# The branch products of a hybrid trunk layer in bursts of half-size products

## The chip, the core and the metric

The kernel runs on one core of a Trainium2 chip. The metric is the device time in microseconds of one execution. The core has TensorE (PE) for matmuls, VectorE (DVE), ScalarE (ACT) and GpSimd (POOL) for elementwise work, and SyncE (SP), which here only issues transfers. SP, ACT and POOL each issue transfers into a queue of their own; POOL's can add into the destination while they write (an accumulating transfer).

## The reference

One layer on x of 1024 tokens x 1024 channels. xn = RMSNorm(x) is projected by one wide matrix; three mixers (a: gMLP, b: RG-LRU, c: SSD) make ya, yb, yc of 1024 x 1024 from it, and three gates come from the same projection. What the change touches is the merge behind the mixers:

```python
merged = (gates[:, :, 0] * jnp.einsum('bse,ed->bsd', ya, w_branch_a[l])
          + gates[:, :, 1] * jnp.einsum('bse,ed->bsd', yb, w_branch_b[l])
          + gates[:, :, 2] * jnp.einsum('bse,ed->bsd', yc, w_branch_c[l]))
h = h + jnp.einsum('bsd,de->bse', merged, w_out[l])
```

The gates are sigmoids; the kernel stores tanh(g/2) and uses (tanh + 1) / 2. Behind the merge come the output projection, a second norm, the MLP relu(. W1)^2 W2, and a last norm. All values are float32.

## The kernel before

Products in float32 accuracy are made of two reduced-precision parts: every operand is split into a high part (ScalarE copies into float32r) and a low part (the source minus the high part), and a product takes three matmuls: high x high, high x low, low x high. The low part is made by VectorE (`split`, L132 and L133) or, for weights of whole units, by ScalarE negating the high part and POOL adding the source with an accumulating transfer (`wtile`, L526 to L528).

Stages in order: the norm and the first projections; 48 units of projection and the mixers; the gates; the branch products; the output projection; the MLP up and down. A unit (`one_unit`) makes 128 output channels x 1024 tokens in a bank pair `ps`: 8 input blocks x 3 parts x 2 halves of the tokens = 48 matmuls of 128x512 (`product`, L555), then its `post` function. `queue` holds the units, and weights are fetched two units ahead.

The gates, the MLP up and the MLP down are already made another way: as a 2x2 block product in seven products instead of eight (the Strassen-Winograd forms). With A the left operand and B the right one in quarters, S1 = A21 + A22, S2 = S1 - A11, S3 = A11 - A21, S4 = A12 - S2, and T1 to T4 likewise of B; seven products A11 B11, A12 B21, S1 T1, S2 T2, S3 T3, S4 B22, A22 T4 give all quarters by additions. `seventh` (L478) makes one product of 12 matmuls (4 input blocks x 3 parts), either starting a bank or adding to what stands in it, so that some of the additions are made by PSUM.

The gate stage runs by pairs of 128 channels (`GatePair`, bursts p1, p2, p5, p6, p3, p7, p4 of 12 matmuls). The last pair's p4 must wait until L958 has read the bank it adds to. Gates go to memory (`gd`, L960 and L966), as the mixers' results do (`yd`).

The branch stage before: 24 units, 8 for each of c, b, a. `load_next` fetches and splits the rows of y for the next branch while the current one runs; `post` (in `branch_unit`) multiplies the gate plus one with the bank (L1050), POOL or VectorE adds to `merged` (L1055, L1057), and with the last branch the sum is halved and split into the operand `M` of the output projection (L1061, L1062). The gates are fetched on the ACT queue, one per unit.

The order within an engine is that of the code inside `tc.manual_schedule()`; elsewhere, and where blocks meet, a scheduler places ready instructions of the next block ahead of waiting ones. Every buffer belongs to a pool of a few equal tiles (`act` 15, `act1` 12, `act3` 16, `w` 6, `raw` 2), and a tile's next use waits for the last reader of the one before. `aux` and `aux2` are four PSUM banks each.

Of the kernel before, what the change touches and what calls it, by code (L numbers as in the profile page):

```python
# [36 lines left out]
def trunk_kernel(ctx: ExitStack, tc: tile.TileContext, x, norm_mix_g, w_in, b_gate, gmlp_ln_g, gmlp_ln_b,  # L37
# [54 lines left out]
    def hsl(h):  # L92
        return slice(h * HF, h * HF + HF)
# [927 lines left out]
    def fetch(b, k):  # L1021
        new = act3 if b == "b" else (act if k < 3 else act1)
        h_, l_ = new(dt=F32R), new(dt=F32R)
        nc.sync.dma_start(out=l_.bitcast(F32), in_=yd[b][k])
        return h_, l_

    Y = {b: Whole([], []) for b in "cba"}
    M = Pairs(act3)

    def load_next(b, k, fetched=None):  # L1030
        h_, l_ = fetched or fetch(b, k)
        split(h_, l_, l_.bitcast(F32))
        Y[b].p[0].append(h_)
        Y[b].p[1].append(l_)

    gate_order = [(b, br, e) for b, br in (("c", 2), ("b", 1), ("a", 0)) for e in range(KD)]
    gates_in = []

    def next_gate():
        if gate_order:  # L1040
            b, br, e = gate_order.pop(0)
            t = act1() if b == "c" and e < 2 else act()
            nc.scalar.dma_start(out=t, in_=gd[br][e])
            gates_in.append(t)

    def branch_unit(b, br, w, e, nxt):
        def post(ps):
            next_gate()
            t = gates_in.pop(0)
            stt(out=t, in0=t, scalar=1.0, in1=ps, op0=ALU.add, op1=ALU.mult)  # L1050
            if b == "c":
                merged.append(t)
            else:
                if b == "b":
                    nc.gpsimd.tensor_tensor(out=merged[e], in0=merged[e], in1=t, op=ALU.add)  # L1055
                else:
                    tt(out=t, in0=merged[e], in1=t, op=ALU.add)  # L1057
                    for half in range(2):
                        tv = t[:, hsl(half)].rearrange("p (c l) -> p c l", c=4)
                        h_, l_ = M.rhs(0, e, half), M.rhs(1, e, half)  # L1060
                        actv(h_, tv, AF.Copy, scale=0.5)  # L1061
                        stt(out=l_, in0=tv, scalar=0.5, in1=h_.bitcast(F32), op0=ALU.mult, op1=ALU.subtract)  # L1062
            if nxt:
                load_next(nxt, e)
        unit(w[0][:, e * P:(e + 1) * P], Y[b], post)

    merged = []
    for b, br, w, nxt in (("c", 2, w_branch_c, "b"), ("b", 1, w_branch_b, "a"), ("a", 0, w_branch_a, None)):
        for e in range(KD):
            branch_unit(b, br, w, e, nxt)  # L1070

    z, prev = cur.pop(), None
    with tc.manual_schedule():
        z.w.cast22()
        while z:
# [6 lines left out]
            if nxt:  # L1082
                nxt.w.cast1()
            else:
                ahead(1)
                early = [fetch("c", 0), fetch("c", 1)]
            z.p5()
            if nxt:
                nxt.w.sums1()
            z.p6()  # L1090
            if nxt:
                nxt.w.sums2()
                nxt.w.cast12()
            else:
                early.append(fetch("c", 2))
                load_next("c", 0, early[0])
                ahead(2)
            z.p3()
            if nxt:
                nxt.w.cast22()  # L1100
            else:
                load_next("c", 1, early[1])
            z.p7()
            if not nxt:
                load_next("c", 2, early[2])
            prev, z = z, nxt
        prev.p4()
    del prev, z, nxt, early
    XF.clear()
    gatep.close()  # L1110
    wide = ExitStack()
    mainp = wide.enter_context(tc.tile_pool(name="mainps2", bufs=2, space=bass.MemoryType.PSUM, reuse_waits="tile"))
# [4 lines left out]
    with tc.manual_schedule():  # L1117
        early = [fetch("c", k) for k in range(3, KD)]
        for k in range(3, KD):
            load_next("c", k, early[k - 3])  # L1120
        next_gate()
        one_unit()
    del early
    run()
    Y.clear()
    merged.clear()
    mixers.close()
    acts.close()
    pools[0] = ctx.enter_context(tc.tile_pool(name="act2", bufs=27, reuse_waits="tile"))
    wide.close()  # L1130
    aux2p = ctx.enter_context(tc.tile_pool(name="aux2ps", bufs=4, space=bass.MemoryType.PSUM))
# [3 lines left out]


# [12 lines left out]
    wo = [[], []]  # L1149
    for nb in range(2):  # L1150
        for k2 in range(4):
            raw = rawp.tile([P, 2, HF], F32, tag="raw", name=nm("raw"))
            nc.sync.dma_start(out=raw, in_=w_out[k2 * 256:k2 * 256 + 256, hsl(nb)].rearrange("(k p) e -> p k e", p=P))
            hi, lo = w_pair(nb == 0 and k2 < 3)
            split(hi, lo, raw)
            wo[nb] += [(hi[:, k, :], lo[:, k, :]) for k in range(2)]
# [11 lines left out]
    for cp in range(NCH // 2):  # L1168
        pss = [aux(), aux()]
        if cp:  # L1170
            for i in range(2):
                residual(2 * cp + i)
        for ks in (range(KD - 1), (KD - 1,)):
            for i in range(2):
                out_products(pss[i], 0, 2 * cp + i, ks)
        for i in range(2):
# [458 lines left out]
```

## Time and profile before

| what | value |
|---|---|
| median of 3 runs | 2013.63 us (2012.44 to 2013.72) |
| the profiled execution, as timed | 2012.43 us |
| its span | 2010.6 us |
| PE busy | 1957.1 us, 97% |
| VectorE, ScalarE busy | 60%, 48% |
| branch stage, first to last matmul | 1005.2 to 1266.8 us |
| data moved | 285.54 MB, mean 142 GB/s |

The page lists the busy time of each engine, then what ended the idle time ahead of each group of instructions. A group is named by line, engine and operation, output <- inputs and shape; L478 and L555 are helper lines which many stages share, so a stage is found by its window. PEld is the weight load that goes with each matmul. A row of the windows view gives start and end, its length, then busy time and count for PE, PEld, DVE, ACT and POOL, the granted clock of TensorE, the busy share of the 16 transfer engines and GB/s. Rows of the transfer queues give packets, MB and the share of the time of the 16 engines; q1 and q10 serve SP and ACT, q0 serves POOL. The granted clock was 1.00 in the whole branch stage.

### The profile page before, as it was taken

The page shows a single profiled execution, that of the slowest core. Times are in us where ns is not written, and L with a number is a line of the kernel's source. Part 1 is how long each engine was busy: PE and PEld are TensorE (multiplying, and loading weights), DVE is VectorE, ACT ScalarE, POOL GpSimd, SP SyncE. Part 2 cuts the span into 40 slices and gives each one's busy share as a digit, 9 for nine tenths or more (in the row PEclk, how much of TensorE's full clock was granted, in tenths as well). Part 3 has the DMA queues.
Part 4 walks back from the last instruction along what each step waited for, and adds up shares of the span by engine and source line. Part 5 has one row for each costly group of instructions (what it writes and reads, how often), then busy time and mean ns, then how long its engine had stood idle before and what let it go on. Part 6 is the DMA issues. An engine that isn't in the chain of part 4 may idle for free.

```text
span 2010.6 us, 23918 instructions
## 1 busy us (share of the span) xinstructions
PE 1957.1 (97%) x9156; PEld 1629.6 (81%) x9156; DVE 1215.9 (60%) x1795; ACT 955.3 (48%) x1385; POOL 327.3 (16%) x410
## 2 busy tenths in 40 slices
PE   8999999999999999999999999998999999999996
PEld 7998878788788787888788888887788887888885
DVE  5485766776767678444423123336666557787787
ACT  6424665756656634444533222156555555253243
POOL 4112222331322432000000320000111110000000
PEclk9999999999999999999999999999999999999998
DMA  4246447356355654333597654421544448544632
GB/s 158 67 138 149 99 113 159 91 132 135 95 119 117 157 140 133 116 105 115 166 316 184 157 145 131 158 94 53 167 162 140 159 154 307 188 138 135 188 112 88
DMA packets 214887, 285.54 MB, mean 142 GB/s; under 512 B 12548, under 2 KB 149972, under 8 KB 214772
## 3 DMA queue, kind: packets, MB, share of 16 engines
q1 hardware_dynamic: 175636, 144.91, 24.1%
q0 software_dynamic: 33200, 117.59, 22.5%
q10 hardware_dynamic: 5936, 21.51, 3.2%
q8 instruction: 72, 1.18, 0.2%
q14 instruction: 43, 0.35, 0.1%
HBM read 178.97 MB, written 67.24 MB: 122 GB/s over the span
## 4 chain that ended last, share of the span: by engine, by line
PE 83%; DVE 11%; ACT 4%; issue 2%; POOL 1%; ACTq 0%; DVEq 0%; POOLq 0%
PE ps L555 34%; PE aux L478 29%; PE gps L478 8%; PE aux L257 4%; PE aux L1166 3%; PE aux L816 1%; PE aux L735 1%; PE aux L731 1%; DVE a L578 1%; ACT a L1206 1%; DVE a L831 1%; DVE h L752 1%; DVE rsq_q L111 1%; DVE a L702 0%; DVE a L133 0%
## 5 line engine op out<-in xcount | busy, mean ns | idle before, releaser
L555 PE MATMUL ps<-xn,wh 128*128 128x512 f32 x1536 | 418.3, 392 | 0.0
L555 PEld LDWEIGHTS ps<-xn,wh 128*128 128x128 f32 x1536 | 286.8, 188 | 61.2 <-issue 2.8
L555 PE MATMUL ps<-xn,wl 128*128 128x512 f32 x768 | 236.6, 389 | 0.0
L478 PE MATMUL aux<-a,b 128*128 128x512 f32 x864 | 197.3, 389 | 0.0
L478 PEld LDWEIGHTS aux<-a,b 128*128 128x128 f32 x864 | 162.2, 188 | 33.7
L526 ACT ACTIVATE wh<-raw 128x1024 fp32r<-128x1024 f32 x72 | 76.1, 1057 | 214.7 <-PE ps L555 203.7
L555 PEld LDWEIGHTS ps<-xn,wl 128*128 128x128 f32 x768 | 144.2, 188 | 30.2
L478 PE MATMUL aux<-b,wt 128*128 128x512 f32 x672 | 156.9, 389 | 0.0
L478 PEld LDWEIGHTS aux<-b,wt 128*128 128x128 f32 x672 | 126.2, 188 | 26.1
L528 POOL DMA_DIRECT2D wl<-raw x72 | 63.6, 883 | 393.6 <-ACT wl L527 232.8
L478 PE MATMUL aux<-b,b 128*128 128x512 f32 x480 | 110.6, 389 | 0.0
L1387 DVE TENSOR_TENSOR a<-aux,a 128x512 f32<-128x512 f32 x112 | 77.0, 688 | 50.4 <-PE aux L478 50.4
L133 DVE TENSOR_TENSOR wt<-a,wt 128x1024 fp32r<-128x1024 f32 x52 | 63.7, 1226 | 72.3 <-ACT wt L132 72.3
L478 PE MATMUL gps<-xn,wt 128*128 128x512 f32 x432 | 103.8, 394 | 2.1 <-DVE a L238 2.1
L1050 DVE SCALAR_TENSOR_TENSOR a<-a,ps 128x1024 f32<-128x1024 f32 x22 | 26.8, 1220 | 130.2 <-PE ps L555 117.4
L478 PEld LDWEIGHTS aux<-b,b 128*128 128x128 f32 x480 | 90.1, 188 | 18.7
L478 PEld LDWEIGHTS gps<-xn,wt 128*128 128x128 f32 x432 | 82.1, 190 | 19.6 <-issue 2.5
L133 DVE TENSOR_TENSOR a<-a,a 128x1024 fp32r<-128x1024 f32 (+1 forms) x65 | 66.7, 1033 | 49.1 <-ACT a L132 49.1
L132 ACT ACTIVATE b<-wt 128x1024 fp32r<-128x1024 f32 x60 | 61.9, 1053 | 69.7 <-DMA wt<-u_d 63.8
L555 PE MATMUL ps<-c,wh 128*128 128x512 f32 x320 | 85.5, 389 | 0.0
L478 PE MATMUL aux<-a,wt 128*128 128x512 f32 x336 | 80.0, 395 | 3.3 <-ACT a L1264 3.3
L132 ACT ACTIVATE a<-a 128x1024 fp32r<-128x1024 f32 (+1 forms) x65 | 55.8, 874 | 55.7 <-DVE a L1339 44.4
(333 smaller groups left out, 3687.0 us busy)
## 6 DMA issues: line engine op xcount, KB each, us to landing
wl<-raw POOLq DMA_DIRECT2D x72, 512.0 KB, 5.1
wt<-u_d SPq DMA_DIRECT2D x54, 512.0 KB
raw<-in_w_in_dram SPq DMA_DIRECT2D x48, 512.0 KB
u_d<-a POOLq DMA_DIRECT2D x48, 512.0 KB, 5.2
g_d<-a POOLq DMA_DIRECT2D x24, 512.0 KB, 2.9
a<-g_d ACTq DMA_DIRECT2D x22, 512.0 KB
rt<-in_w_mlp_up_dram SPq DMA_DIRECT2D x17, 512.0 KB
a<-acs_d POOLq DMA_DIRECT2D x32, 256.0 KB, 8.0
```

The source lines that it names most:

```text
L111: stt(out=q, in0=r, scalar=nh, in1=r, op0=ALU.mult, op1=ALU.mult)
L132: actv(dst_hi, src, AF.Copy)
L133: (eng or nc.vector).tensor_tensor(out=dst_lo, in0=src, in1=dst_hi.bitcast(F32), op=ALU.subtract)
L257: mm(ps[:, :nt], X.tok(a, k, c), wk[k][w], start=(k == 0 and i == 0), stop=(k == KD - 1 and i == 2))
L478: mm(ps, lhs[l][kk], rhs[r][kk], start=(new and n == 0), stop=(n == 11), skip_group_check=not new)
L526: actv(hi, raw, AF.Copy)
L528: nc.gpsimd.dma_start(out=lo, in_=raw, accum_op=ALU.add)
L555: mm(ps[:, hsl(h)], w[wi][:, k, :], a.rhs(ai, k, h), start=(n == 0), stop=(n == 3 * KD - 1))
L578: stt(out=dst[:, j:], in0=ps[:, :T - j], scalar=taps[3 - j], in1=dst[:, j:], op0=ALU.mult, op1=ALU.add)
L1050: stt(out=t, in0=t, scalar=1.0, in1=ps, op0=ALU.add, op1=ALU.mult)
L1166: mm(ps, M.tok(a, k, c), wo[nb][k][w], start=(k == 0 and a + w == 0), stop=(k == KD - 1 and a == 1))
L1387: tt(out=h, in0=ps, in1=h, op=ALU.add)
```

## The change

The 24 units give way to three branches of seven bursts. A burst is one of the seven half-size products: A is w of the branch (transposed use: 512 input channels x 512 output channels), B is y (512 input channels x 512 tokens). It runs in four positions p of 128 output channels, 12 matmuls each, so a burst is 48 matmuls into four banks. The order is A12 B21, A11 B11, S1 T1, S4 B22, S2 T2, S3 T3, A22 T4. Bursts 0 and 2 start the four `aux` banks, burst 1 starts the four `aux2` banks; burst 3 adds to burst 2's, bursts 4, 5 and 6 add to burst 1's. After bursts 0, 2 and 3 ScalarE copies each bank to SBUF (`prior`), after the others VectorE reads it (`collect`), adds a `prior` where one belongs, and multiplies with the gate's quarter (512 channels x 512 tokens, loaded by `gate_load` as 256 x 512 each).

`make` prepares the next burst's four operand halves, one per position: a high copy on ScalarE, a low half on VectorE, and the sums. The signs differ a little from the textbook: S is loaded as A21, A22 is added from memory by an accumulating transfer, later ScalarE negates it and a transfer adds A11; that sum is then added into A12 by two more. A22 of each branch is split with an accumulating transfer instead of VectorE (`split_dma`).

The merge goes by quarters: the products of c stay in `merged`, b's are added into them (two quarters by accumulating transfers, two by VectorE), a's get them added, and `to_operand` makes M. The first weights of the output projection are loaded and split during the last two bursts (`wo_load`, `wo_make`), and its first half now stands in a block with a manual order. A DMA on SP or ACT waits for a free buffer in its place in the queue.

```diff
+    BRANCHES = (("c", 2, w_branch_c), ("b", 1, w_branch_b), ("a", 0, w_branch_a))
+    ORDER = (("A12", "B21"), ("A11", "B11"), ("S1", "T1"), ("S4", "B22"), ("S2", "T2"), ("S3", "T3"), ("A22", "T4"))
+    NM = len(BRANCHES) * len(ORDER)
...
+    def add_into(out_, in_):
+        nc.gpsimd.dma_start(out=out_, in_=in_, accum_op=ALU.add)
+
+    def sums_load(b):
+        w_load(b, "A21", w4, "S")
+        for h in range(2):
+            add_into(L[b, "S"][h], w_view(b, "A22", h))
+
+
+    def split_dma(hi, lo, src):
+        actv(hi, src, AF.Copy)
+        actv(lo, hi.bitcast(F32), AF.Copy, scale=-1.0)
+        add_into(lo, src)
...
+    def make(b, i, s):
+
+        side, h = (s // 2) ^ (i == 3), s % 2
+        new = op_new(b, i, side)
+        pr = OP.setdefault((b, i), ([], []))[side]
+        if side == 0:
+            src = L[b, ("A12", "A11", "S", "A12", "S", "A21", "A22")[i]][h]
+            hi, lo = new(two, F32R), new(two, F32R)
+            (split_dma if i == 6 else split)(hi, lo, src)
+            if i == 2:
+                actv(src, src, AF.Copy, scale=-1.0)
+                add_into(src, L[b, "A11"][h])
+                for k in range(2 * h):
+                    add_into(L[b, "A12"][k], L[b, "S"][k])
+            elif i == 4:
+                t = L[b, "A21"][h]
+                tt(out=t, in0=L[b, "A11"][h], in1=t, op=sub)
+        elif i == 0:
...
+        else:
+            hi, lo = new(two, F32R), new(two, F32R)
+            split(hi, lo, R[b, ("", "B11", "B11", "B22", "B11", "B12", "B21")[i]][h])
+            r = lambda name: R[b, name][h]
+            if i == 1:
+                tt(out=r("B11"), in0=r("B12"), in1=r("B11"), op=sub)
+            elif i == 3:
+                tt(out=r("B11"), in0=r("B11"), in1=r("B22"), op=sub)
+                tt(out=r("B12"), in0=r("B22"), in1=r("B12"), op=sub)
+            elif i == 4:
+                tt(out=r("B21"), in0=r("B21"), in1=r("B11"), op=ALU.add)
+        pr.append((hi, lo))
...
+    def to_operand(q, j, t):
+        eh, th = q
+        tv = t.rearrange("p k (c l) -> p k c l", c=4)
+        h_, l_ = M.tile(0, th, 2 * eh + j), M.tile(1, th, 2 * eh + j)
+        actv(h_, tv, AF.Copy, scale=0.5)
+        stt(out=l_, in0=tv, scalar=0.5, in1=h_.bitcast(F32), op0=ALU.mult, op1=ALU.subtract)
...
+    def collect(b, r, p, ps):
+        j, s = divmod(p, 2)
+        if r in (0, 2, 3):
+            if s == 0:
+                prior[b, r, j] = act1(two)
+            actv(prior[b, r, j][:, s], ps, AF.Copy)
+            return
...
+    def merge_product(n, p):
+        b, r = divmod(n, 7)
+        if r in (0, 2):
+            mps[r, p] = aux()
+        elif r == 1:
+            mps[1, p] = aux2()
+        ps = mps[(0, 1, 2, 2, 1, 1, 1)[r], p]
+        lhs, rhs = ([[pr[kk // 2][part][:, kk % 2] for kk in range(4)] for part in range(2)] for pr in OP[b, r])
+        lhs = [[o[:, p * P:(p + 1) * P] for o in part] for part in lhs]
+        seventh(ps, lhs, rhs, r < 3)
+        if p == 0:
+            loads(b, r)
+        if n + 1 < NM:
+            make(*divmod(n + 1, 7), p)
+        if b == 2 and (r, p) in ((5, 1), (5, 3), (6, 1)):
+            wo_make(0, (5, 5, 6).index(r) + (p == 3), True)
+        d = defer.pop((n, p), None)
+        if d:
+            d()
+        collect(b, r, p, ps)
...
     with tc.manual_schedule():
-        early = [fetch("c", k) for k in range(3, KD)]
-        for k in range(3, KD):
-            load_next("c", k, early[k - 3])
-        next_gate()
-        one_unit()
...
+    with tc.manual_schedule():
+        for n in range(NM):
+            for p in range(4):
+                merge_product(n, p)
...
+    with tc.manual_schedule():
+        for cp in range(NCH // 2):
+            pss = [aux(), aux()]
...
+            if cp == 0:
+                for i in range(2):
+                    out_products(pss[i], 0, i, range(6))
+                wo_make(0, 3)
+                for i in range(2):
+                    out_products(pss[i], 0, i, (6, 7))
+                wo_make(1, 0)
+            else:
+                for i in range(2):
+                    out_products(pss[i], 0, 2 * cp + i, range(KD))
+                wo_make(1, cp)
```

On TensorE, where the gates end and the branches begin (aux is the first branch bank, gps the last gate burst, ps the first branch unit), before:

```order
L478 MATMUL gps_7839<-xn_540,wt_7855 128x512
L478 MATMUL gps_7839<-a_6150,a_7821 128x512
L478 MATMUL gps_7839<-a_6151,a_7821 128x512
...
L478 MATMUL gps_7839<-a_6432,a_7821 128x512
L555 MATMUL ps_8039<-a_7894,wh_7889 128x512 x2
L555 MATMUL ps_8039<-a_7895,wh_7889 128x512 x2
```

and now:

```order
L478 MATMUL gps_7839<-xn_540,wt_7855 128x512
L478 MATMUL aux_8019<-a_7915,a_7953 128x512
L478 MATMUL aux_8019<-a_7891,a_7953 128x512
L478 MATMUL aux_8019<-a_7915,a_7954 128x512
L478 MATMUL aux_8019<-a_7915,a_7953 128x512
L478 MATMUL gps_7839<-a_6150,a_7821 128x512
...
L478 MATMUL gps_7839<-a_6432,a_7821 128x512
L478 MATMUL aux_8019<-a_7891,a_7953 128x512
L478 MATMUL aux_8019<-a_7915,a_7954 128x512
```

Four matmuls of the first branch burst now stand ahead of the last gate burst p4.

On POOL in the changed kernel, the transfers of branch c (wt_7931 and wt_7932 are the two halves of S, wt_7895 and wt_7896 those of A11, rt those of A12, b_8450 and b_8468 the low halves of A22):

```order
L1061 DMA wt_7931<-in_w_branch_c_dram 128x2x512
L1061 DMA wt_7932<-in_w_branch_c_dram 128x2x512
L960 DMA g_d<-a_7852 128x1024
L966 DMA g_d<-a_7912 128x1024
L1061 DMA wt_7931<-wt_7895 128x1024
L1061 DMA wt_7932<-wt_7896 128x1024
L1061 DMA rt_7887<-wt_7931 128x1024
L1061 DMA rt_7888<-wt_7932 128x1024
L1061 DMA b_8450<-wt_8359 128x1024
L1061 DMA b_8468<-wt_8360 128x1024
```

Before, POOL made one transfer per unit here (L528) and added the products of b (L1055); the chain S, then A12, is new, and the two stores of the last gates stand between its first steps.

On VectorE, from the low half of S (second burst) to that of A12 (third burst), in the changed kernel:

```order
L1187 SCALAR_TENSOR_TENSOR a_8034<-a_8034,c_8078 128x1024
L133 TENSOR_TENSOR b_8205<-c_8112,b_8204 128x1024
L1111 TENSOR_TENSOR c_7989<-c_7989,c_8112 128x1024
L1112 TENSOR_TENSOR c_7993<-c_8112,c_7993 128x1024
L133 TENSOR_TENSOR b_8226<-c_8113,b_8225 128x1024
L1111 TENSOR_TENSOR c_7990<-c_7990,c_8113 128x1024
L1112 TENSOR_TENSOR c_7994<-c_8113,c_7994 128x1024
L133 TENSOR_TENSOR b_8246<-rt_7887,b_8245 128x1024
L133 TENSOR_TENSOR b_8265<-rt_7888,b_8264 128x1024
```

The eight rows behind the first are VectorE's work in the third burst; the last two read the A12 that the transfers have added to. Before, VectorE had one read of a bank pair (L1050) and at most one low half per unit here.

On TensorE, at the start of the last burst (aux_1341 is a branch bank, aux_9813 the first bank of the output projection, wb its weights):

```order
L478 MATMUL aux_1341_9255<-c_9662,a_9613 128x512
L1313 MATMUL aux_9813<-wb_9636,b_9426 128x512
L1313 MATMUL aux_9813<-wb_9637,b_9426 128x512
L1313 MATMUL aux_9813<-wb_9636,b_9427 128x512
...
L478 MATMUL aux_1341_9255<-c_9663,a_9613 128x512
L478 MATMUL aux_1341_9255<-c_9662,a_9614 128x512
```

Six matmuls of the output projection, which before followed the last unit, stand behind the first matmul of the last burst.

More of the change, by code (lines that the diff above doesn't have):

```diff
@@ new lines, in loads @@
+    def loads(b, r):
+        if r == 0:
+            gate_load(b, 0, 0)
+            if b:
+                sums_load(b)
+                y_load(b, "B12")
+        elif r == 1:
+            y_load(b, "B22")
+        elif r == 2:
+            w_load(b, "A21", w4)
+            y_load(b, "B21")
+        elif r == 3:
+            gate_load(b, 0, 1)
+        elif r == 4:
+            w_load(b, "A22", w4)
+            gate_load(b, 1, 1)
+            if b == 2:
+                wo_load(0, 0)
+                wo_load(0, 1)
+        elif r == 5:
+            gate_load(b, 1, 0)
+            if b < 2:
+                w_load(b + 1, "A12", r4)
+                y_first(b + 1, act1)
+        elif b < 2:
+            w_load(b + 1, "A11", w4)
+            y_load(b + 1, "B11")
@@ L1084, in trunk_kernel @@
             else:
-                ahead(1)
-                early = [fetch("c", 0), fetch("c", 1)]
+                w_load(0, "A12", r4)
+                y_first(0, act)
+                w_load(0, "A11", w4)
             z.p5()
@@ L1101, in trunk_kernel @@
             else:
[L1102 removed]
+                make(0, 0, 0)
             z.p7()
             if not nxt:
[L1105 removed]
+                make(0, 0, 1)
             prev, z = z, nxt
[L1107 to L1112, printed above, removed]
+    for n in list(XF):
+        if n != "T4":
+            del XF[n]
     mixers.close()
```

166 lines of the change are left out of this document (95 added, 71 removed).

## The prediction

> **What bounds the kernel now.** I read the page first, then the chain of waits from 980 us on, the timeline of TensorE at both ends of the branch stage, the groups by shape in that stage, and busy time and transfers by window. All come from the profiled execution (span 2010.6 us, 2012.43 us as timed).
>
> ```profile
> PE 1957.1 (97%) x9156; PEld 1629.6 (81%) x9156; DVE 1215.9 (60%) x1795; ACT 955.3 (48%) x1385; POOL 327.3 (16%) x410
> PE 83%; DVE 11%; ACT 4%; issue 2%; POOL 1%; ACTq 0%; DVEq 0%; POOLq 0%
> ```
>
> TensorE is the bound, so a change is worth what it does to TensorE's count of matmuls or to its gaps. The chain through the stage:
>
> ```profile
> 992.24 2.73 PE gps L478 x12
> ...
> 1001.45 3.03 PE gps L478 x12
> 1004.50 0.70 ACT a L928
> 1005.24 261.70 PE ps L555 x1152
> 1266.93 54.41 PE aux L1166 x240
> ```
>
> The 1152 matmuls of the three branch products stand as one piece: nothing interrupts them, and the output projection follows at once. A group of 12 takes 2.73 us, 0.227 us a matmul, the same in the gate stage (L478) and here (261.70 / 1152). The timeline shows the only gaps, at entry:
>
> ```profile
> 1001.45 3.01 PE L478 MATMUL gps<-a,a 128*128 128x512 f32 x12 [1.05 <-DVE a L958]
> 1005.24 1.21 PE L555 MATMUL ps<-a,wh 128*128 128x512 f32 x4 [0.78 <-ACT a L928]
> ...
> 1266.77 10.13 PE L1166 MATMUL aux<-wb,b 128*128 128x512 f32 x44
> ```
>
> **The matmuls.** Each branch goes from 8 units of 48 matmuls (384) to 7 bursts of 4 x 12 (336); the order of the changed program has 1008 for the three. Its operands have the shapes of the gate stage, so I keep that price: 1008 x 0.227 = 228.8 us, and the 144 that go are worth 144 x 0.227, that is **-32.7 us**. That the halves of a bank are now written by 12 matmuls in a row instead of 48 alternating ones is what the gate bursts do too, at the same rate.
>
> **The entry.** The last gate burst must wait until L958 has read its bank; now four ready matmuls of the first branch burst stand ahead of it and fill 4 x 0.227 = 0.9 of the 1.05 us. The 0.78 us goes altogether: it is the wait for a gate bank that the old wide pool took over, while the new first burst writes the auxiliary banks. **-1.7 us** (bounds 0 and -1.83).
>
> **VectorE and ScalarE.** The new work has these prices:
>
> ```profile
> L133 DVE TENSOR_TENSOR b<-b,b 128x1024 fp32r<-128x1024 f32 x8 | 9.8, 1225 | 29.0 <-ACT b L132 28.9
> L132 ACT ACTIVATE b<-b 128x1024 fp32r<-128x1024 f32 x8 | 8.5, 1059 | 27.2 <-DMA b<-yb_d 27.2
> L1050 DVE SCALAR_TENSOR_TENSOR a<-a,ps 128x1024 f32<-128x1024 f32 x22 | 26.8, 1220 | 130.2 <-PE ps L555 117.4 <-issue 12.8
> L954 DVE TENSOR_TENSOR a<-aux,a 128x512 f32<-128x512 f32 x11 | 7.6, 691 | 0.0
> L945 ACT ACTIVATE a<-aux 128x512 f32<-128x512 f32 x11 | 6.6, 599 | 19.1 <-PE aux L478 19.1
> 1005.00:1267.00 262.00, 261.76 (x1154) 216.51 (x1154) 70.42 (x66) 77.00 (x82) 38.23 (x31) 1.00 0.66 181
> 1760.00:1800.00 40.00, 40.00 (x178) 33.11 (x177) 34.79 (x38) 20.71 (x21) 0.00 (x0) 1.00 0.46 147
> ```
>
> Per branch VectorE makes 26 low halves, 10 sums of blocks and 6 gate products of 128x1024, and 16 reads of banks of 128x512; the second and third branches add 14 of 128x1024 for merging. That is 140 x 1.22 + 48 x 0.69 = 204 us, 89% of 228.8, up from 70 of 262. ScalarE: some 110 x 1.06 + 36 x 0.60 = 138 us, 60%. The nearest row is the down projection (last one above), with the same bursts: VectorE 87% busy and TensorE never idle. So the average fits, and the question is the boundary between bursts. The tightest is the fourth burst of a branch. In the third, VectorE issues eight operations of 1.22 us (9.8) after a carry of about 2.1 us from the second (0.69 + 1.22 behind its last bank): 11.9 us. A burst lasts 48 x 0.227 = 10.9 us; the last of the eight is read first by matmul 9 of the next, 8 x 0.227 = 1.8 us on, at 12.7. It has 0.8 us to spare, if its sources are there. The other boundaries have 1.4 us or more. Cost **0**; if that cover were gone, up to about 1 us at each of three boundaries.
>
> **Chained transfers.** What comes late is decided by the accumulating transfers that POOL issues (the first line is of the whole kernel, median to landing last):
>
> ```profile
> wl<-raw POOLq DMA_DIRECT2D x72, 512.0 KB, 5.1
> ...
> L528 POOL DMA_DIRECT2D wl<-raw x22: 847/858/890, 1015.7 to 1236.3; - x22
> DMA to landing us min/median/max: 4.5/6.8/9.2
> L1239 POOL DMA_DIRECT2D u_d<-a x39: 710/710/722, 1440.9 to 1672.5; - x39
> 1440.00:1660.00 220.00, 220.00 (x973) 182.21 (x971) 132.13 (x174) 117.21 (x174) 32.69 (x48) 1.00 0.45 156
> ```
>
> Per branch: S is negated in place by ScalarE during the second burst, A11 is added into it by a transfer, and that sum is added into A12 by a second transfer, for two halves each, in one queue, where the second kind waits for the first to land. Count from the start of the second burst. The first negation is done at 4.2 us (copy 1.06, low half 1.22, negation 1.06, behind a bank copy of 0.6), the second at 7.5. With 6.8 us to land the four arrive at 11.0, 14.3, 17.9 and 21.2. The last feeds a copy and a low half: done at 23.5, read at 10.9 + 12.7 = 23.6. So the chain just fits at the median of this stage; at 4.5 us it has over 4 us to spare; at 9.2 the four arrive at 13.4, 16.7, 22.6 and 26.0, and the matmul waits 4.7 us. What waits first is ScalarE's copy of A12; behind it stand two bank copies, which nobody reads for two bursts, and the halves of the next burst, which then start late but have 1.4 us and the 4.7 us of the stopped TensorE to catch up. While the chain runs, SP and ACT have little to load (B21 at its start), so I take the better half: **+0.5 us** per branch, +1.5 in all (bounds 0 and +14). S itself is made by an accumulate that reads A22 from memory. No row shows one; it is issued a whole burst (10.9 us) or more ahead of its reader, so the 9.2 of the nearest row is hidden.
>
> **Exit.** The out weights come during the last two bursts through the same queue. TensorE's order puts six output matmuls behind the first matmul of the last burst, and the second of them needs the transferred low half. It is issued 5.2 to 5.8 us into the burst before (ScalarE waits some 2 to 2.6 us for a merge that is landing, then three copies of 1.06), and with 5.1 to 6.8 us it lands at 10.3 to 12.6 against 10.9 + 2 x 0.227 = 11.3 needed: 0 to 1.3 us, taken as **+0.5**. The last merged rows take 0.69 + 1.22 + 1.06 + 1.22 = 4.2 us behind the last bank; 29 matmuls (6.6 us) of earlier rows cover that. Behind it the program is the same, and its weights wait only for raw buffers that come free some 20 us early.
>
> The sum: -32.7 - 1.7 + 1.5 + 0.5 = -32.4 us. 2012.43 - 32.4 = 1980.0 as timed; the median of the runs shown, 2013.63, is 1.2 above the profiled execution: **1981.2 us**. The term of the matmuls alone carries it.
>
> **Rivals.**
>
> *Late chain.* Every chained accumulate takes 9.2 us, by other traffic or because POOL's issue waits behind a VectorE instruction now that VectorE is 89% busy. Then it costs 3 x 4.7, and the exit its 1.3, instead of 2.0 in all: 1981.2 + 13.4 = 1994.6 us. For it: 9.2 has been seen in this stage. Against: POOL issued u_d in 710 to 722 ns with VectorE at 132 of 220 us, without a spread. The Trainium skill, "SBUF — State Buffer", section "Who interferes with whom", has the rule that speaks for it: a transfer stalled by a VectorE instruction is one whose descriptors GpSimd writes, starved of the shared port. By that rule, one VectorE instruction of 1.22 us lost per transfer, the chain would be 2 x 1.22 later and the sum about 3 x 2.3 = 7 us higher; the row of u_d shows nothing of it, at lower load.
>
> *Transfers as the bound.* The stage now has 84 plain transfers and 37 accumulates, 121 x 0.524 = 63.4 MB, in the 228.8 us and the last gate burst of 2.7, some 232 us (273 GB/s, before 181).
>
> ```profile
> DMA packets 33272, 47.54 MB, mean 181 GB/s; under 512 B 1472, under 2 KB 24000, under 8 KB 33260
> q1 hardware_dynamic: 26334, 22.21, 26.6%
> q0 software_dynamic: 3566, 12.97, 24.7%
> q10 hardware_dynamic: 3360, 12.19, 14.5%
> ...
> 1010.00:1015.00 5.00, 5.00 (x24) 4.14 (x23) 0.62 (x1) 2.12 (x2) 0.00 (x0) 1.00 1.06 397
> ...
> 1020.00:1025.00 5.00, 5.00 (x24) 4.14 (x23) 1.23 (x1) 0.25 (x1) 0.32 (x1) 1.00 1.05 273
> ```
>
> At the rates per busy time of these queues (34.4 MB in 41.1% of 262 us is 319 GB/s for the hardware queues, 12.97 MB in 24.7% is 200 for the accumulates) that is 44.0 / 0.319 + 19.4 / 0.200 = 235 us, 3 us over TensorE's 232, and with uneven demand perhaps 8: 1984 to 1989, say 1987 us. Against: with all engines busy the stage moved 273 to 397 GB/s, and TensorE ran on.
>
> *Slower than before: the accumulates do not overlap.* If each of the 37 waits for the one before to land, the queue takes 37 x 9.2 = 340 us, 108 more than 232: 2089 us. The point where it decides is 37 x 7.2 = 267 us, where the gain is eaten (232 + 34.4); the median of 6.8 lies close below. For it: in this stage the 22 accumulates are issued 10 us apart (1015.7 to 1236.3), so no row shows two in flight. Against:
>
> ```profile
> 173.84 2.51 POOL L665 DMA_DIRECT2D a<-acs_d  x4
> a<-acs_d POOLq DMA_DIRECT2D x32, 256.0 KB, 8.0
> ```
>
> Four plain transfers of that queue were issued within 2.5 us and landed after 8.0 in the median, so the queue holds several.
>
> That the change removes fewer matmuls than it says is no rival: the order shows them.
>
> **How the numbers follow.** The forecast, 1976 to 1986, has 0.64; the late chain 0.14; transfers as the bound 0.13; no overlap 0.04; 0.05 stays for what I don't see. 8 times in 10 means down to 1976 (no stall, and a better exit) and up to the late chain, 1995. About 0.2% (4 us) is what a measurement here can tell from no change: faster 0.93 (the first three and half of the rest), same 0.02, slower 0.05.
>
> **What would show it.** Right: a branch stage of about 231 us from the last gate burst to the first row of the output projection, 48 matmuls in 10.9 us, VectorE near 89%, TensorE idle in it below 3 us. The late chain: idle TensorE ahead of the fourth burst of each branch, released by VectorE L133 behind a copy that waited for L1061. Transfers: a busy share near 1 throughout, with waits for loads at many bursts. No overlap: landings of accumulates that follow each other at their full length. Wrong in the matmuls: more than 0.227 us each.

## The result and the profile after

| | median, us | range |
|---|---|---|
| before | 2013.62 | 2012.44 to 2013.72 |
| after | 1994.93 | 1993.84 to 1997.11 |
| predicted | 1981.2 | 1976.0 to 1995.0 |

The ratio is 0.991, with a 95% interval of 0.9893 to 0.9927: faster, by 18.7 us where 32.4 were forecast. The page of the profiled execution (1994.12 us as timed, span 1992.4), busy time and then the chain of waits:

```profile
PE 1928.5 (97%) x9012; PEld 1603.6 (80%) x9012; DVE 1329.9 (67%) x1908; ACT 998.8 (50%) x1440; POOL 321.9 (16%) x415
PE 76%; DVE 10%; DMA 5%; ACT 4%; issue 4%; POOL 1%; SPq 0%; ACTq 0%; DVEq 0%; POOLq 0%
```

The 144 matmuls are gone (9156 to 9012). New in the chain is DMA with 5%: before, no transfer stood in it.

To measure the stage alone, take the start of the last gate burst and the first transposes (128x128) behind the first output products. Between these two TensorE runs the same program in all kernels here but for the branch products. TensorE's timeline, one row of before and two of after:

```profile
1323.89 1.04 PE L1201 MATMUL aux<-ident,a 128*128 128x128 f32 x8
```

```profile
1001.46 3.02 PE L478 MATMUL gps<-a,a 128*128 128x512 f32 x12
...
1306.93 1.03 PE L1357 MATMUL aux<-ident,a 128*128 128x128 f32 x8
```

Before it is 1323.89 - 1001.45 = 322.4 us, after 1306.93 - 1001.46 = 305.5: 17.0 less. The matmuls and the entry alone were to bring 34.4, so the stage itself lost about 17.4 us, and what lies ahead of and behind it matters little. The waits of TensorE show where (line, what it waited for: us in total, times, longest), then the gaps in its timeline:

```profile
PE aux L478 <- DMA b<-wt: 6.6, 3, 3.5
PE aux L1313 <- DMA wb<-rt: 5.2, 2, 4.5
```

```profile
1072.28 9.38 PE L478 MATMUL aux<-b,b 128*128 128x512 f32 x40 [1.40 <-DMA b<-wt]
...
1150.94 2.15 PE L478 MATMUL aux<-b,b 128*128 128x512 f32 x6 [3.55 <-DMA b<-wt]
1154.73 11.23 PE L478 MATMUL aux<-b,b 128*128 128x512 f32 x40 [1.64 <-DMA b<-wt]
...
1236.23 2.50 PE L1313 MATMUL aux<-wb,b 128*128 128x512 f32 x5 [4.54 <-DMA wb<-rt]
```

Two things are late, both made by an accumulating transfer. `b<-wt` is the low half of A22, for the seventh burst of the first two branches (c and b). `wb<-rt` is the low half of an out weight, at the exit. Together 11.8 us. The count of matmuls beside the durations shows a second loss: the 40 matmuls behind the gap of 1.40 us took 9.38, the 40 behind 3.55 and 1.64 took 11.23. Windows ahead of and around the gaps of branch b, and behind the large gap at the exit:

```profile
1132.00:1144.00 12.00, 12.00 (x54) 9.94 (x54) 8.52 (x10) 6.04 (x6) 3.43 (x4) 1.00 1.06 338
1144.00:1156.00 12.00, 6.81 (x24) 4.73 (x24) 6.54 (x7) 4.85 (x5) 0.70 (x1) 0.83 1.05 292
...
1236.00:1240.00 4.00, 3.77 (x9) 2.99 (x10) 0.16 (x1) 1.06 (x1) 0.60 (x1) 0.50 1.04 193
```

The granted clock (third column from the end), 1.00 everywhere in this stage before, is 0.83 over the 12 us around the gaps of branch b and 0.50 at the exit. The transfer engines are full there (share 1.04 to 1.06). The chain (start, us, what) and the transfers of 1000 to 1240 us:

```profile
1047.83 9.99 DMA a<-g_d
...
1062.82 9.41 DMA b<-wt
...
1141.43 13.25 DMA b<-wt
...
1225.81 10.38 DMA wb<-rt
1236.25 9.25 DMA rt<-in_w_out_dram
```

```profile
DMA packets 27235, 60.31 MB, mean 251 GB/s; under 512 B 1830, under 2 KB 1830, under 8 KB 27222
q0 software_dynamic: 6086, 19.40, 41.6%
q1 hardware_dynamic: 14608, 28.15, 33.9%
...
wt<-wt POOLq DMA_DIRECT2D x6, 512.0 KB, 4.9
rt<-wt POOLq DMA_DIRECT2D x6, 512.0 KB, 5.4
b<-wt POOLq DMA_DIRECT2D x4, 512.0 KB, 10.5
```

The same kind of transfer of the same 512 KB takes 4.9 to 5.4 us in the third and fourth burst of a branch (`wt<-wt`, `rt<-wt`) and 10.5 in the sixth and seventh (`b<-wt`; 13.25 at worst), when SP fetches the next branch and ACT the last gates.

### The profile page after: what moved, and what is told of

The parts are those of the page before. It is cut to its first block, busy times and chain, and to the rows that moved or that the text cites. A ratio compares the mean times of both kernels' runs of the same rounds, so it can differ in the third digit from the quotient of the medians.

```text
span 1992.4 us, 23855 instructions
## 1 busy us (share of the span) xinstructions
PE 1928.5 (97%) x9012; PEld 1603.6 (80%) x9012; DVE 1329.9 (67%) x1908; ACT 998.8 (50%) x1440; POOL 321.9 (16%) x415
## 4 chain that ended last, share of the span: by engine, by line
PE 76%; DVE 10%; DMA 5%; ACT 4%; issue 4%; POOL 1%; SPq 0%; ACTq 0%; DVEq 0%; POOLq 0%
PE aux L478 35%; PE ps L555 22%; PE gps L478 8%; PE aux L257 3%; PE aux L1313 3%; DMA b<-wt 1%; DMA a<-g_d 1%; PE aux L816 1%; PE aux L735 1%; PE aux L731 1%; DVE a L578 1%; DMA wb<-rt 1%; ACT a L1362 1%; DVE a L831 1%; DVE b L133 1%
## 5 line engine op out<-in xcount | busy, mean ns | idle before, releaser
L478 PE MATMUL aux<-b,b 128*128 128x512 f32 x1152 | 267.0, 392 | 6.6 <-DMA b<-wt 6.6
L478 PEld LDWEIGHTS aux<-b,b 128*128 128x128 f32 x1152 | 217.4, 189 | 53.8 <-DMA b<-wt 8.2
L478 PE MATMUL aux<-a,b 128*128 128x512 f32 x960 | 219.4, 389 | 0.0
L478 PEld LDWEIGHTS aux<-a,b 128*128 128x128 f32 x960 | 180.2, 188 | 37.4
L132 ACT ACTIVATE b<-wt 128x1024 fp32r<-128x1024 f32 x84 | 86.8, 1054 | 71.1 <-DMA wt<-u_d 61.7
L133 DVE TENSOR_TENSOR b<-wt,b 128x1024 fp32r<-128x1024 f32 x84 | 102.4, 1220 | 17.3 <-ACT b L132 17.2
L526 ACT ACTIVATE wh<-raw 128x1024 fp32r<-128x1024 f32 x48 | 50.8, 1058 | 102.3 <-PE ps L555 72.1
L133 DVE TENSOR_TENSOR a<-a,a 128x1024 fp32r<-128x1024 f32 (+1 forms) x61 | 61.9, 1021 | 38.9 <-ACT a L132 38.9
L528 POOL DMA_DIRECT2D wl<-raw x48 | 42.9, 895 | 248.9 <-ACT wl L527 116.3
L578 DVE SCALAR_TENSOR_TENSOR a<-ps,scw,a 128x1023 f32<-128x1023 f32 (+2 forms) x48 | 61.1, 1273 | 32.8 <-ACT a L576 32.1
```

Of the source, the lines that this page charges most:

```text
L132: actv(dst_hi, src, AF.Copy)
L133: (eng or nc.vector).tensor_tensor(out=dst_lo, in0=src, in1=dst_hi.bitcast(F32), op=ALU.subtract)
L478: mm(ps, lhs[l][kk], rhs[r][kk], start=(new and n == 0), stop=(n == 11), skip_group_check=not new)
L526: actv(hi, raw, AF.Copy)
L528: nc.gpsimd.dma_start(out=lo, in_=raw, accum_op=ALU.add)
L578: stt(out=dst[:, j:], in0=ps[:, :T - j], scalar=taps[3 - j], in1=dst[:, j:], op0=ALU.mult, op1=ALU.add)
```

## The experiments

All are the changed kernel with an edit. "Stage" is the stretch measured above.

| kernel | median, us (range) | stage, us | ratio to before, 95% interval |
|---|---|---|---|
| after | 1994.93 (1993.84 to 1997.11) | 305.5 | 0.991 (0.9893 to 0.9927) |
| A22 by VectorE | 1977.71 (1977.28 to 1978.51) | 288.3 | 0.9819 (0.9805 to 0.9832) |
| out weights by VectorE | 1991.50 (1989.43 to 1992.52) | 300.9 | 0.9886 (0.9872 to 0.9899) |
| both by VectorE | 1978.49 (1977.64 to 1980.55) | 288.6 | 0.9824 (0.981 to 0.9837) |
| gate loads behind the copies | 1998.18 (1995.73 to 1999.86) | 309.2 | 0.9917 (0.9904 to 0.9931) |
| half of the gates not loaded | 1992.86 (1991.87 to 1995.54) | 304.2 | 0.9901 (0.9886 to 0.9916) |
| and lighter next loads | 1989.51 (1988.29 to 1990.04) | 299.3 | 0.9881 (0.9867 to 0.9896) |
| VectorE, 2 operations more | 1983.26 (1981.64 to 1984.07) | 292.9 | 0.985 (0.9836 to 0.9865) |
| VectorE, 4 operations more | 1994.85 (1993.64 to 1995.15) | 304.8 | 0.9909 (0.9893 to 0.9926) |
| A22 of branch a by VectorE | 1987.61 (1985.28 to 1989.46) | 297.3 | 0.9871 (0.9856 to 0.9886) |
| A22 of c and b by VectorE | 1984.92 (1983.57 to 1986.57) | 296.7 | 0.9856 (0.984 to 0.9873) |

### Taking the transfers away: A22, the out weights, both

```diff
-            (split_dma if i == 6 else split)(hi, lo, src)
+            split(hi, lo, src)
```

> The low half of A22, the operand of the seventh burst of each branch, is made by VectorE (copy by ScalarE, subtraction by VectorE) instead of a negated copy and an accumulating transfer; the out weights keep their transfers. Theory (the accumulating transfer of A22 is what the last bursts wait for, issued late and landing in 9 to 13 us): the three waits for b<-wt, 6.6 us, go, and with them the slow TensorE behind the gaps of branch b, where 46 matmuls took 13.2 us instead of 46 x 0.227 = 10.4, 2.8 us: 1994.9 - 9.4 = 1985.5 us. The wait of the out weights at the exit (5.2 us) stays. Rival (VectorE takes over as the bound of that boundary: two more operations of 1.22 us in the sixth burst of each branch): the same stops, now released by VectorE L133, 1992 to 1995 us.

```diff
-            wo_make(0, (5, 5, 6).index(r) + (p == 3), True)
+            wo_make(0, (5, 5, 6).index(r) + (p == 3), False)
```

> The low halves of the first three pairs of out weights are made by VectorE instead of accumulating transfers; A22 keeps its transfers. Theory (the exit waits for that transfer, 10.4 us to land, and for the raw buffer that it holds): the waits for wb<-rt, 5.2 us, go, and with them the slow clock of 0.50 to 0.92 behind the gap, some 2.2 us: 1994.9 - 7.4 = 1987.5 us; the three waits for b<-wt stay. Rival (the raw out weights themselves, rt<-in_w_out at 9.25 us, are late at the exit whoever splits them): the wait stays with another name, 1992 to 1996 us.

The third kernel has both.

> Both edits together: A22 and the out weights are split by VectorE. Theory (the two lots of transfers are all that went wrong): the waits and the slow clock behind them go, 9.4 + 7.4 = 16.8 us, 1994.9 - 16.8 = 1978.1 us, and TensorE has no gap over 0.5 us in the branch stage. Rival (nine more operations of VectorE, 11 us, in a stage where it is 77 to 82% busy, make new gaps): 1983 to 1990 us with TensorE waiting for L133.

With A22 alone on VectorE the stage has one gap left in TensorE's timeline (first and last row of the stretch, and the gap; then the chain of waits that ends at this gap):

```profile
1000.91 3.02 PE L478 MATMUL gps<-a,a 128*128 128x512 f32 x12
...
1037.66 42.04 PE L478 MATMUL aux<-b,b 128*128 128x512 f32 x184 [0.18 <-DVE b L133]
...
1289.23 1.04 PE L1357 MATMUL aux<-ident,a 128*128 128x128 f32 x8
```

```profile
1021.44 8.11 DMA wt<-wt
...
1030.07 5.19 DMA rt<-wt
...
1036.38 1.24 DVE b L133
```

The stage takes 288.3 us, 34.1 less than before, against the 34.4 of the matmuls and the entry. The theory's mechanism holds, its size does not: 17.2 us came back where 9.4 were expected, because the exit's wait went too. The rival, VectorE as the new bound, did not appear: the one gap, 0.18 us ahead of the ninth matmul of branch c's fourth burst, is released by VectorE, but VectorE had itself waited for the chained transfers S to A12. The out weights alone gave 3.4 of 7.4 us: their wait went, but three shorter ones stood in its place at the exit (1.85 us together, for a merged row and for an out weight split later), which is the rival in part, and the waits for A22 stayed, at 7.0 us. Both edits together land on their theory (1978.5 against 1978.1 us), but they add nothing to the first alone.

### Why the exit went with A22: one branch at a time

```diff
-            (split_dma if i == 6 else split)(hi, lo, src)
+            (split_dma if i == 6 and b < 2 else split)(hi, lo, src)
```

The second kernel has `b == 2` in place of `b < 2`.

> VectorE splits A22 in the last branch (a) alone; the first two branches keep the transfers of A22, and the out weights keep theirs. In the changed kernel the two transfers of this A22, 1.05 MB, are issued 2 us ahead of the out weights' on the same queue. Theory (the exit is late since these two go ahead of the out weights through full engines, so that taking A22 alone away mended both): the waits for b<-wt stay at about 6.6 us with their slow clock, those for wb<-rt at the exit (5.2 us, and some 2.2 us of slow clock) go: 1994.9 - 7.4 = 1987.5 us. Rival (the exit of the kernel with all of A22 on VectorE was on time because the whole branch came 8 us sooner against loads that run on their own time): the exit's wait stays at 3 us or more, 1992 to 1995 us.

> The counterpart: VectorE splits A22 in the first two branches, the last branch keeps the two transfers of A22 ahead of the out weights'. Theory: the waits for b<-wt and the slow clock behind them go, 9.4 us, the exit waits for wb<-rt as before, 5.2 us and some 2.2 of slow clock: 1994.9 - 9.4 = 1985.5 us. Rival (as above, the exit depends on when the branch comes): no wait at the exit, 1978 us.

Waits of TensorE for transfers, first kernel, then second:

```profile
PE aux L478 <- DMA b<-wt: 6.6, 3, 3.4
PE aux L1313 <- DMA wb<-rt: 0.3, 1, 0.3
```

```profile
PE aux L1313 <- DMA wb<-rt: 5.2, 2, 4.7
```

Each edit removes its own half: 1987.6 and 1984.9 us, within 0.6 us of the theory, and the two gains (7.3 and 10.0) add up to 17.3, against 17.2 for all three branches. So the exit was late because of branch a's A22, not because of when the branch came. Two things come with it: two negated copies on ScalarE ahead of the out weight's, and two transfers ahead of the out weight's on the same queue. Without them the first out weight's transfer is issued 2.0 us sooner in its burst and lands after 7.4 us instead of 10.4; the two shares were not tested apart. That branch has no wait for its own A22 in the changed kernel, but it hands the delay on: the first out weight lands late, holds its raw buffer, the third raw weight is fetched late (the 9.25 us in the chain above), and its transfer follows.

### Started too late, or too long under way

ScalarE's queue issues two pairs of gate loads in the fifth and sixth burst, and the second pair holds ScalarE until an earlier load has landed, just ahead of A22's copies. If that hold makes A22 late, moving the issues helps.

```diff
         elif r == 4:
             w_load(b, "A22", w4)
-            gate_load(b, 1, 1)
...
         elif r == 5:
-            gate_load(b, 1, 0)
...
             make(*divmod(n + 1, 7), p)
+        if r in (4, 5) and p == 3:
+            gate_load(b, 1, 5 - r)
```

> Only the place of two gate loads on ScalarE's queue changes: those of the fifth and sixth burst of each branch are issued at the end of their burst, behind the copies for the next operands, instead of at its start; all transfers stay. Theory (ScalarE is held at these issues until an earlier gate load has landed, so that the copies of A22 and its transfer start late): the transfers of A22 start about 3 us sooner, the waits for b<-wt fall from 6.6 to 0 to 2 us, and some of the slow clock goes: 1994.9 - 7 = 1988 us. Rival (the transfer engines are full in these stretches, and what is issued sooner lands no sooner): the landings of b<-wt grow by as much as they start sooner, 1993 to 1997 us.

The theory fell: 1998.2 us, if anything slower. ScalarE's first copy of A22 in branches c and b, in the changed kernel and in this one (start, us, what, idle before and what ended it):

```profile
1058.33 1.06 ACT L1070 ACTIVATE b<-wt 128x1024 fp32r<-128x1024 f32 x1 [6.14 <-PE aux L478]
...
1136.94 1.07 ACT L1070 ACTIVATE b<-wt 128x1024 fp32r<-128x1024 f32 x1 [6.86 <-DMA a<-g_d]
```

```profile
1058.19 1.06 ACT L1070 ACTIVATE b<-wt 128x1024 fp32r<-128x1024 f32 x1 [4.95 <-issue]
...
1135.64 1.07 ACT L1070 ACTIVATE b<-wt 128x1024 fp32r<-128x1024 f32 x1 [4.96 <-issue]
```

```profile
b<-wt POOLq DMA_DIRECT2D x4, 512.0 KB, 11.3
```

```profile
PE aux L478 <- DMA b<-wt: 5.6, 3, 3.6
```

Counted from the last gate burst (1001.46 and 1002.65 us), the copy starts 1.3 us sooner in branch c and 2.5 us sooner in b, and the hold by the gate load is gone in both. (The row of the changed kernel names TensorE in c, but the chain above has the gate load there, landed at 1047.83 + 9.99 = 1057.8 us, just ahead of the copy.) In the edited kernel TensorE is the next limit: in c ScalarE stands at a semaphore from 1051.5 us until a matmul in the last quarter of the fifth burst ends, 6.66 us later, presumably since the copy takes the buffer that it reads. What started sooner landed hardly sooner: the landings grew from 10.5 to 11.3 us in the median (the last row ahead of the waits), and the waits for A22 fell by 1.0 us, not by 5 to 7. That is the rival. The exit got worse, with a wait of 7.8 us. Whether one more operand buffer would start the transfer early enough was not tried.

The other half of the question is how long the transfer is under way. In the next two kernels work is left out: half of the gates are not loaded, and then of two operands for the next branch only one half is loaded and used twice.

```diff
+            if eh:
+                continue
             e = 4 * eh + 2 * j
             nc.scalar.dma_start(out=t, in_=gd[BRANCHES[b][1]][e:e + 2, :, hsl(th)].rearrange("e p t -> p e t"))
...
+            actv(g[:, s], ps, AF.Copy)
             stt(out=g[:, s], in0=g[:, s], scalar=1.0, in1=ps, op0=ALU.add, op1=ALU.mult)
...
-                stt(out=g, in0=g, scalar=1.0, in1=t, op0=ALU.add, op1=ALU.mult)
+                stt(out=g, in0=t if q[0] else g, scalar=1.0, in1=t, op0=ALU.add, op1=ALU.mult)
```

> The changed kernel with A22's transfers as they are, but the gates of the lower half of the rows are not loaded (their products are made with another operand; the merged rows of that half are therefore not those of the reference). It takes 4 of the 8 gate loads of a branch away, 2.1 MB, all of them issued in the fifth and sixth burst, where ScalarE's queue held 20 to 21% of the transfer engines' time. Theory (the transfers of A22 land late since they share full engines with loads): with a fifth of the demand gone the landings of 9.4 to 13.3 us become 7.5 to 10.5, the waits for b<-wt fall from 6.6 us to about 2, with less slow clock behind them: 1994.9 - 4 to 7 = 1988 to 1991 us. Rival (an accumulating transfer takes this long by itself, two at a time): landings and waits stay, 1993 to 1997 us.

```diff
+        if b and name == "B11":
+            R[b, name] = R[b, name][:1] * 2
-        for h, t in enumerate(R[b, name]):
+        for h, t in enumerate(R[b, name][:1 if b and name == "B11" else 2]):
...
+        if b:
+            R[b, "first"] = R[b, "first"][:1] * 2
...
```

> As the kernel before it in this list, and of B11 and the first B21 of the second and third branch only one half is loaded and used twice (the products of these branches are therefore not the reference's): 1.05 MB less of the SP queue's loads for each of them, in the stretch in which A22's transfers of the branch before are under way. Theory (full engines): a third of the demand of that stretch is gone, landings of 6 to 8 us, no wait for b<-wt over 0.5 us, the exit's wait for wb<-rt unchanged or smaller: 1994.9 - 9 = 1986 us or less. Rival (the accumulating transfer by itself): waits stay at 5 to 7 us, 1993 to 1997 us.

Median landing of A22's transfers and TensorE's waits for them, first kernel, then second:

```profile
b<-wt POOLq DMA_DIRECT2D x4, 512.0 KB, 9.3
```

```profile
PE aux L1316 <- ACT b L1152: 5.2, 1, 5.2
PE aux L478 <- DMA b<-wt: 3.0, 2, 2.0
PE aux L478 <- DMA a<-wt: 0.7, 1, 0.7
```

```profile
b<-wt POOLq DMA_DIRECT2D x4, 512.0 KB, 7.0
```

```profile
PE aux L478 <- DMA b<-wt: 1.1, 1, 1.1
PE aux L478 <- DMA a<-wt: 0.8, 1, 0.8
```

With less beside it the same transfer lands after 10.5, 9.3 and 7.0 us in the median, and the waits for A22 fall from 6.6 to 3.7 and 1.9 us (with branch a's own, `a<-wt`, which had none in the changed kernel). Part of that is no shorter landing but an earlier start, as these gate loads no longer hold ScalarE either. The second half of branch b's A22 keeps the two apart. With all loads but the gates behind the copies, with half of the gates left out, and with the lighter next loads as well, it is issued 9.3 us before TensorE would have read it each time, and it lands after 15.5, 13.2 and 10.4 us. The rival, that it takes this long by itself, is out; the engines it shares with loads set its time. The times gained less than expected (2.1 us, which the ranges hardly tell from nothing, and 5.4 us, against 4 to 7 and 9): the exit's delay stayed. Its place is another one, since in these two kernels the scheduler put the whole last burst ahead of the output products, and its name is that of the merged rows, which stand in ScalarE's queue behind the late third out weight (5.2 and 5.4 us). There the traffic is POOL's own, which neither edit lightens; the queues of the changed kernel from 1232 to 1244 us:

```profile
q0 software_dynamic: 585, 2.11, 98.6%
```

### The boundary that was called the tightest, and the clock

A22 stays on VectorE here, and VectorE makes two (then four) low halves of the third burst again.

```diff
+        if i == 3 and s in (0, 2):
+            tt(out=lo, in0=(L[b, "A12"] if s else R[b, "B22"])[h], in1=hi.bitcast(F32), op=sub)
```

> The kernel with A22 split by VectorE (1977.7 us), and in the third burst of each branch VectorE makes two low halves a second time: 2 x 1.22 = 2.44 us more in the burst ahead of the boundary that the prediction called the tightest (0.8 us to spare by its count; the run shows a gap of 0.18 us there). Theory (the boundary decides, not the average): TensorE stops at the seventh to ninth matmul of the fourth burst of each branch for 1.6 to 2.6 us, released by VectorE: 3 x 2.1 = 6 us, 1984 us, and no slow clock behind gaps of this size. Rival (the average decides: VectorE idles a fifth of the time and absorbs 2.44 us): 1977 to 1979 us.

> As the kernel before it in this list, with four low halves made again instead of two: 4.88 us more. Theory (the boundary decides, and a gap of some 3.5 us and more is followed by a slow clock that costs about 2 us, as behind the gaps of 3.55 and 4.54 us): gaps of 4.0 to 5.0 us in each branch, a granted clock below 1 behind each, 1977.7 + 3 x 4.6 + 3 x 2 = 1997 us. Rival (the clock has nothing to do with the gaps): 1977.7 + 3 x 4.6 = 1991.5 us with the clock at 1.00 throughout the stage.

TensorE's timeline in the fourth burst of the three branches, two operations more, then four:

```profile
1039.50 43.36 PE L478 MATMUL aux<-b,b 128*128 128x512 f32 x190 [1.22 <-DVE b L1116]
1117.17 43.37 PE L478 MATMUL aux<-b,b 128*128 128x512 f32 x190 [1.22 <-DVE b L1116]
1195.34 10.73 PE L478 MATMUL aux<-b,b 128*128 128x512 f32 x46 [1.71 <-DVE b L1116]
```

```profile
1039.57 44.82 PE L478 MATMUL aux<-b,b 128*128 128x512 f32 x190 [3.74 <-DVE b L1117]
1121.22 44.94 PE L478 MATMUL aux<-b,b 128*128 128x512 f32 x190 [3.74 <-DVE b L1117]
1203.49 12.14 PE L478 MATMUL aux<-b,b 128*128 128x512 f32 x46 [4.23 <-DVE b L1117]
```

The window behind the last of these gaps:

```profile
1204.00:1208.00 4.00, 4.00 (x14) 3.12 (x13) 3.98 (x4) 0.51 (x2) 0.00 (x0) 0.68 0.07 9
```

2.44 us more of VectorE stopped TensorE for 1.22, 1.22 and 1.71 us. So 1.2, 1.2 and 0.7 us of it fitted in at this boundary, and VectorE's idle fifth elsewhere absorbs nothing: 1983.3 us, where the theory said 1984 and the rival 1977 to 1979. Four more gave gaps 2.5 us larger, and the groups behind them are slower at the same count: 44.82 against 43.36, 44.94 against 43.37, 12.14 against 10.73. That is 1.5 us behind each gap of some 4 us, with a clock of 0.68, and nothing of it behind 1.2 to 1.7 us. Expected were 1997 with and 1991.5 without the clock; measured 1994.85. The stage's 16.5 us over the kernel without the additions are 11.7 of gaps and 4.4 of clock, within 0.6.

## Why the prediction was wrong, step by step

**Matmuls, -32.7, and entry, -1.7: right.** Where nothing is late (A22 on VectorE) the stage is 34.1 us shorter, against 34.4. At the entry, four matmuls stand ahead of the last gate burst and that burst has no gap.

**VectorE, cost 0 with 0.8 us to spare at the fourth burst: right in place and size.** In the changed kernel the last low half was ready 1.3 us (branch b) and 0.8 us (a) before the ninth matmul started; in c the chained transfer decided, not VectorE. Its work had been counted some 10% too high: 183 us from 1003 to 1245 us in the changed kernel, 75%, where 204 us and 89% were forecast, in the main because its operations follow each other every 1.14 us where 1.22 was taken.

**Chained transfers S to A12, +1.5: too high, with nothing to spare in one branch.** They landed after 4.9 and 5.4 us in the median where 6.8 was taken, and no fourth burst waits for them in the changed kernel. The median hides branch c. There the first kind took 7.9 and 8.4 us, the last transfer arrived 21.3 us after the start of the second burst (21.2 in the prediction's count), and the low half was ready at 1037.89 us for a matmul that started at 1037.94. In b and a the last one arrived after 18.7 and 18.6 us. "While the chain runs, SP and ACT have little to load" holds for b and a; in c loads on SP's queue took 30% of the engines' time from 1018 to 1036 us.

**The step that failed** is the list of transfers that the sum counts, behind "Chained transfers" and "Exit". The low half of A22, an accumulating transfer that the diff shows, has no term in the sum. It was the wrong one to leave out: it starts only some 8 us ahead of its reader (the second half in branch c is issued at 1062.82 us and was wanted at 1070.9), when the next branch is being loaded. It cost 6.6 us of waits at the seventh bursts. The exit, taken as +0.5 with a landing of 5.1 to 6.8 us, cost 5.2: the first out weight's transfer landed after 10.4, behind A22's, although it was issued 5.6 us into its burst, as the prediction had it.

**Not foreseen at all** was the clock. In the profiled pair of the changed kernel and the one with A22 on VectorE, the stage differs by 305.5 - 288.3 = 17.2 us; 11.8 are gaps, and the rest, 5.4, is the slow TensorE behind them (1.85 of it in the one group of 40 matmuls above). So of the missing 15.4 us in the stage (32.4 forecast, 17.0 measured), waits beyond the 2.0 counted are 9.8 and the clock 5.4, within 0.2.

**The rivals.** The late chain's 1994.6 us is the time that was measured, but that is a coincidence, and so is the measured time's place just inside the stated range: its transfers were on time, in branch c barely, and its mark, idle TensorE ahead of the fourth bursts, is absent. Transfers as the bound (1984 to 1989) was nearest in kind: the share of the engines is near 1 for long stretches, 60.3 MB at 251 GB/s against 63.4 at 273 forecast. It was priced as an average over the stage, 3 to 8 us, with waits at many bursts. The waits came at three places, where transfers issued 6 to 8 us ahead of their readers met full engines. The row quoted as evidence against it, TensorE running on at 273 and 397 GB/s, came from a stage in which weights are fetched two units, 21.8 us, ahead. No overlap (2089) is out: A22's two transfers were issued 2 us apart and both were under way.

The Trainium skill, "SBUF — State Buffer", section "Who interferes with whom", was weighed at 7 us: VectorE holding up the descriptors that GpSimd writes. POOL issued the chained transfers in 849 to 888 ns with VectorE at three quarters and more, as it did before at 847 to 890, so nothing here shows that cost.

## What to carry to other kernels

List every transfer that a matmul reads, with the time from the earliest moment its source and its buffer are there to its reader, and price each at the load of that stretch, not at the median of the stage; those that land later than their lead allows decide. An accumulating transfer that saves VectorE 1.2 us is a bad trade where its lead is a single burst and VectorE has room at that boundary: giving these six back is the best version here, 1977.7 us. A gap of several us in TensorE cost 1.4 to 2.2 us more than its length here (the same 46 matmuls took 12.14 and 10.73 us behind gaps of 4.23 and 1.71 us; at the exit the 11 behind 4.54 us took 2.2 us longer than with A22 on VectorE).

## What was not expected of the hardware

The clock does not need a long gap. Behind two gaps of 1.97 and 1.02 us, six matmuls apart (half of the gates not loaded), 40 matmuls took 11.47 us, and the clock stood at 0.50:

```profile
1152.34 11.47 PE L478 MATMUL aux<-b,b 128*128 128x512 f32 x40 [1.02 <-DMA b<-wt]
```

```profile
1152.00:1156.00 4.00, 3.66 (x9) 2.89 (x10) 0.69 (x1) 1.54 (x2) 0.00 (x0) 0.50 1.10 261
```

Single gaps of 1.22 to 1.71 us had no such effect, and one of 2.6 us had it in one kernel and not in the other. It stands at the same 24 matmuls behind the output projection, before (clock 0.64 in the next 4 us) and after (1.00):

```profile
1429.15 7.07 PE L478 MATMUL aux<-a,wt 128*128 128x512 f32 x24 [2.56 <-ACT a L1264]
```

```profile
1412.25 5.76 PE L478 MATMUL aux<-a,wt 128*128 128x512 f32 x24 [2.57 <-ACT a L1420]
```

What decides it no run here shows. The Trainium skill, "TensorE: Matmul & The Clock Gate", section "HAM oscillation — how this bites in real kernels", puts the limit at idle gaps over about 3.4 us; the gaps of 3.55 to 4.54 us agree with it; the pair, 3.0 us in all, and the 2.56 us lie below.

Bytes do not tell how full the transfer engines are: at a share of 1.0 they moved 338 GB/s in one of the windows above and 193 in another, where POOL's accumulating transfers made up most of the traffic. By the rows of the queues, q0 moved 19.40 MB in 41.6% and q1 28.15 MB in 33.9% of the same 240 us: 194 against 346 GB/s of busy time.
